# Weight halves side by side and packed operand rows at fixed distances, in a hybrid decoder trunk on one Trainium2 core

## The chip, the cores and the metric

The kernel runs on one core of one Trainium2 chip. The metric is device time in microseconds (us), the median over executions. A core has TensorE (matmuls; PE in the profile, with PEld for its weight loads), VectorE (DVE), ScalarE (ACT), GpSimd (POOL) and SyncE (SP, which here issues the weight DMAs). TensorE reads both operands of a matmul from SBUF, a memory of 128 partitions, and accumulates in PSUM. An address below is a byte address inside one partition; it is the same in all 128.

## The reference

One decoder layer over 16 learned meta tokens and 256 tokens of width 2,048, in float32. A mixer runs two branches side by side on the normalised input, and a squared-ReLU MLP follows.

```python
def hybrid_mixer(xn, w_in, b_forget, w_alpha2, b_alpha, gla_norm_g, w_o_fox, w_o_gla, w_out):
    proj = xn @ w_in
    ...
    o_fox = forgetting_attention(fq, fk, fv, ff, b_forget)
    g_log = jax.nn.log_sigmoid((ga @ w_alpha2 + b_alpha).astype(jnp.float32)) / GLA_TAU
    o_gla = gated_linear_attention(gq, gk, gv, g_log)
    o_gla = (head_rmsnorm(o_gla, gla_norm_g) * jax.nn.silu(gr.astype(jnp.float32))).astype(xn.dtype)
    y = jax.nn.sigmoid(gate_fox) * (o_fox @ w_o_fox) + jax.nn.sigmoid(gate_gla) * (o_gla @ w_o_gla)
    return y @ w_out

def squared_relu_mlp(xn, w1, w2):
    return jnp.square(jax.nn.relu(xn @ w1)) @ w2

def reference(x, ...):
    h = jnp.concatenate([meta, x], axis=1)
    for l in range(DEPTH):          # DEPTH = 1
        h = h + hybrid_mixer(rmsnorm(h, norm_mix_g[l]), ...)
        h = h + squared_relu_mlp(rmsnorm(h, norm_mlp_g[l]), w_ff1[l], w_ff2[l])
    return rmsnorm(h, final_norm_g)[:, N_META:]
```

All large products are [256 or 272 tokens, 2,048] by a weight matrix; w_ff1 and w_ff2 are 2,048 x 8,192 and 8,192 x 2,048.

## The kernel before

Activations lie transposed: features on the partitions, in KT = 16 row tiles of 128, tokens along the free dimension. Weights come as chunks of [2,048 x 128], each 16 blocks of [128 x 128], one block per row tile k; the function `stream` lists the chunks in the order in which they are used.

Precision. Each float32 number is split into an upper part (rounded to the type fp32r) and a lower part (the rest). A product is upper weights by upper and lower activations, plus lower weights by upper activations. In `gemm2` with `mac2` (lines 135 to 146) that is, for each k, one matmul of 512 columns (line 136: upper block by the row's 256 upper and 256 lower columns) and one of 256 columns (line 137: lower block by the 256 upper columns). The text calls these two a pair. A chunk is 16 pairs into one PSUM bank. `gemm_all` (lines 148 to 157) does the same for all 272 tokens in three matmuls of 272 columns. Every matmul loads its own block of weights, while the one before it runs.

Weights. `weight_half` (line 108) takes half a chunk, eight blocks: a DMA into a tile `raw` (line 118, SyncE's queue), a cast to the upper tile on ScalarE (line 120) and a subtraction to the lower tile on VectorE (line 121). Tiles `raw`, `whi` and `wlo` have five buffers each, so these run ahead of TensorE. In `whi` and in `wlo` the eight blocks lie one behind the other, 512 bytes apart. `first_weights` (line 274) does it for the first seven chunks, in eight stages of two row tiles each, and the two tiles `small` (line 357) hold 40 narrow columns in blocks that POOL fills with zeros first (lines 361 and 362). For the last four chunks the upper part goes to a tile of its own, `whi_last` (line 839).

Operands. `operand` (line 221) lays 16 rows into one tile; row k is a place `at` and a step `gap` from its upper to its lower half, both in elements of four bytes:

```python
    S1, S2 = 8728, 8628
    AT_OG = [(540 * k, 264) for k in range(KT)]
    AT_Y = [(544 * k + 16, 256 + 2 * (k // 2)) for k in range(KT)]
    AT_X2 = [(524 * k, 256) for k in range(KT)]
    AT_A = [(544 * k, 256 + 4 * (k // 2)) for k in range(KT)]
```

Four operands go this way: og (the GLA branch's output, for w_o_gla), y (the gated sum, for w_out), x2 (the MLP's normalised input, for w_ff1) and a (the squared ReLU, for w_ff2, made anew for each of the four groups g of 2,048 hidden features). y and a share the tile s1 with x, the mixer's input, whose rows are 272 + 272 elements; og and x2 share s2. The attention branch's output `of` has eight rows of 512 elements and is not among the four.

Order of the work: GLA heads and then attention heads with their projections (x), eight rounds of four gate chunks (x), one chunk for two column tiles of w_o_fox (of) and two chunks of w_o_gla (og), 16 chunks of w_out (y), and four times 16 chunks of w_ff1 (x2) and 16 of w_ff2 (a). TensorE's order is written out by the program; small matmuls of the branches are put between chunks by `later`.

Of the kernel before, what the change touches and what calls it, by code (L numbers as in the profile page):

```python
# [7 lines left out]
F32 = mybir.dt.float32  # L8
F32R = mybir.dt.float32r
# [7 lines left out]
P = 128  # L17
D = 2048
KT = D // P
NM = 16  # L20
NT = 256
# [44 lines left out]
def trunk(ctx: ExitStack, tc: tile.TileContext, hT, w_small, w_all, consts, w_alpha2, out):  # L66
    nc = tc.nc
    serial = [0]

    def nm(s):  # L70
        serial[0] += 1
        return f"{s}_{serial[0]}"

    const = ctx.enter_context(tc.tile_pool(name="const", bufs=1))
    keep = ctx.enter_context(tc.tile_pool(name="keep", bufs=1))
    wp = ctx.enter_context(tc.tile_pool(name="wp", bufs=5))
# [28 lines left out]
    chunk = [0]  # L105
    HK = KT // 2

    def weight_half(c, i, hi=None):

        raw = wp.tile([P, HK * P], F32, tag="raw", name=nm("raw"), bufs=RAW)  # L110
        if hi is None:
            hi = wp.tile([P, HK, P], F32R, tag="whi", name=nm("whi"))
        lo = wp.tile([P, HK, P], F32R, tag="wlo", name=nm("wlo"))

        def step(k0, n):
            k = slice(k0, k0 + n)
            cols = slice(k0 * P, (k0 + n) * P)
            nc.sync.dma_start(raw[:, cols], w_all[c][:, i * HK * P + cols.start : i * HK * P + cols.stop])
            r = raw.rearrange("p (k m) -> p k m", m=P)[:, k, :]
            nc.scalar.copy(hi[:, k, :], r)  # L120
            nc.vector.tensor_tensor(lo[:, k, :], r, hi[:, k, :].bitcast(F32), op=ALU.subtract)  # L121

        return hi, lo, step

    def next_weights(keep_hi=None):
        c = chunk[0]
        chunk[0] += 1
        parts = []
        for i in range(2):
            hi, lo, step = weight_half(c, i, None if keep_hi is None else keep_hi[:, HK * i : HK * (i + 1), :])  # L130
            step(0, HK)
            parts.append((hi, lo))
        return lambda k: (parts[k // HK][0][:, k % HK, :], parts[k // HK][1][:, k % HK, :])
# [5 lines left out]
    def gemm2(w, x, k0=0, nk=KT):  # L139

        ps = bank(pg, "ps")
        for k in range(nk):
            hi, lo = w(k0 + k)
            mac2(ps, hi, lo, x[k], k == 0, k == nk - 1)
        issued()
        return ps
# [12 lines left out]
    def total(ps, t=None):  # L159

        b = tmp.tile([P, NT], F32, tag="evb", name=nm("evb"))
        nc.scalar.copy(b, ps[:, NT:512])
        if t is None:
            t = tmp.tile([P, NT], F32, tag="evt", name=nm("evt"), bufs=4)
        nc.vector.tensor_tensor(t, ps[:, 0:NT], b, op=ALU.add)  # L165
        return t
# [54 lines left out]
    def operand(pool, name, size, places, tag):  # L221


        t = pool.tile([P, size], F32R, tag=tag, name=nm(name))
        rows = []
        for at, gap in places:
            both = t[:, at : at + 2 * gap].rearrange("p (o t) -> p o t", t=gap) if at + 2 * gap <= size else None
            rows.append(both[:, :, 0:NT])
        return rows

    S1, S2 = 8728, 8628
    AT_OG = [(540 * k, 264) for k in range(KT)]
    AT_Y = [(544 * k + 16, 256 + 2 * (k // 2)) for k in range(KT)]
    AT_X2 = [(524 * k, 256) for k in range(KT)]
    AT_A = [(544 * k, 256 + 4 * (k // 2)) for k in range(KT)]


    h = keep.tile([P, KT, NA + 3], F32, name="h")
# [23 lines left out]
    def gain(i, k):  # L262
        return h[:, k, NA + i : NA + i + 1]
# [9 lines left out]

    def first_weights(c0, n, k0):
        raw = wp.tile([P, HK * P], F32, tag="raw", name=nm("raw"), bufs=RAW)
        hi = wp.tile([P, HK, P], F32R, tag="whi", name=nm("whi"))
        lo = wp.tile([P, HK, P], F32R, tag="wlo", name=nm("wlo"))
        r, hi, lo = (t[:, 0 : 2 * n * P].rearrange("p (c k m) -> p c k m", k=2, m=P)
                     for t in (raw, hi.rearrange("p k m -> p (k m)"), lo.rearrange("p k m -> p (k m)")))

        def load(k, nk):
            nc.sync.dma_start(r[:, :, k : k + nk, :],
                              w_all[c0 : c0 + n, :, (k0 + k) * P : (k0 + k + nk) * P].rearrange("c p (k m) -> p c k m", m=P))

        def cut(k, nk):
            ks = slice(k, k + nk)
            nc.scalar.copy(hi[:, :, ks, :], r[:, :, ks, :])
            nc.vector.tensor_tensor(lo[:, :, ks, :], r[:, :, ks, :], hi[:, :, ks, :].bitcast(F32), op=ALU.subtract)

        return hi, lo, load, cut  # L290
# [12 lines left out]
    def load_stage(s):  # L303
        stages[s] = [first_weights(c0, n, 2 * s) for c0, n in ((0, 4), (4, 3))]
        for k in range(2) if s == 0 else (0,):
            for hi, lo, load, cut in stages[s]:
                load(k, 1 if s == 0 else 2)
# [12 lines left out]
    for s in range(KT // 2):  # L320
# [3 lines left out]
        for kk in range(2):  # L324
            k = 2 * s + kk
# [30 lines left out]

    small = []
    for i in range(2):
        hi = wp.tile([P, HK, P], F32R, tag="whi", name=nm("whi"))
        lo = wp.tile([P, HK, P], F32R, tag="wlo", name=nm("wlo"))  # L360
        nc.gpsimd.memset(hi.bitcast(F32), 0.0)
        nc.gpsimd.memset(lo.bitcast(F32), 0.0)
        ws = wsm[:, HK * i : HK * (i + 1), :]
        nc.scalar.copy(hi[:, :, 0:40], ws)
        nc.vector.tensor_tensor(lo[:, :, 0:40], ws, hi[:, :, 0:40].bitcast(F32), op=ALU.subtract)
        small.append((hi, lo))
# [62 lines left out]
    def og_tile():  # L429
        if not og_box:  # L430
            og_box.append(operand(keep, "og", S2, AT_OG, "s2"))
        return og_box[0]
# [307 lines left out]
    for j0 in range(0, KT, 2):  # L740
        gates = ahead if j0 == 0 else [gate() for _ in range(4)]
        w = next_weights()
        for j in range(2):
            t = total(gemm2(w, oft, k0=8 * j, nk=8))
            nc.vector.tensor_tensor(gates[2 * j], gates[2 * j], t, op=ALU.mult)
        for j in range(2):
            t = total(gemm2(next_weights(), og))
            nc.vector.tensor_tensor(t, gates[2 * j + 1], t, op=ALU.mult)
            nc.vector.tensor_tensor(yf[:, j0 + j, :], gates[2 * j], t, op=ALU.add)
    y = operand(keep, "y", S1, AT_Y, "s1")  # L750
    for j in range(KT):
# [5 lines left out]
    ht = h[:, :, NM:NA]  # L757
    x2 = operand(keep, "x2", S2, AT_X2, "s2")

    def square_sum(j, acc):  # L760
        if j == 0:
            nc.scalar.activation(acc, ht[:, j, :], AF.Square)
        else:
            sq = gat.tile([P, NT], F32, tag="hsq", name=nm("hsq"))
            nc.scalar.activation(sq, ht[:, j, :], AF.Square)  # L765
            nc.gpsimd.tensor_tensor(acc, acc, sq, op=ALU.add)  # L766

    def add_residual(j, ps):
        b = tmp.tile([P, NT], F32, tag="evb", name=nm("evb"))
        nc.scalar.copy(b, ps[:, NT:512])  # L770
        nc.vector.tensor_tensor(ht[:, j, :], ps[:, 0:NT], ht[:, j, :], op=ALU.add)
        nc.vector.tensor_tensor(ht[:, j, :], ht[:, j, :], b, op=ALU.add)
# [37 lines left out]
    def relu2(a, f, ps):  # L810
        t = total(ps)
        nc.vector.scalar_tensor_tensor(t, t, 0.0, r2b, op0=ALU.max, op1=ALU.mult)
        s = gat.tile([P, NT], F32, tag="asq", name=nm("asq"))
        nc.vector.tensor_tensor(s, t, t, op=ALU.mult)
        split_to(a[f][:, 0, :], a[f][:, 1, :], s)

    acc = gat.tile([P, NT], F32, tag="acc", name="acc3", bufs=1)
    for g in range(NG):
        a = operand(keep, "a", S1, AT_A, "s1")
        held = []  # L820
        for f in range(KT):
            ps = gemm2(next_weights(), x2)
            if g == 0 and f == 0:
                held.append(ps)
                continue
            if g == 0 and f == 1:
                relu2(a, 0, held.pop())
            relu2(a, f, ps)
        last = g == NG - 1
        for j in range(KT - NL if last else KT):  # L830
            add_residual(j, gemm2(next_weights(), a))
            if last:
                square_sum(j, acc)
                nc.scalar.activation(ht[:, j, :], ht[:, j, :], AF.Identity, scale=gain(2, j))
                if j == 0:
                    tc.keep_in_program_order(nc.scalar.preload_act_table_set("sqrt_and_others"))


    whi = keep.tile([P, NL, KT, P], F32R, tag="s2", name="whi_last")
# [45 lines left out]
    v, p, none = nc.vector, nc.gpsimd, lambda: None  # L885
# [72 lines left out]
```

## Time and profile before

| | |
|---|---|
| median of 3 runs | 1,637.53 us (1,634.11 to 1,637.98) |
| span of the profiled execution, first to last instruction | 1,632.3 us |
| TensorE busy | 1,614.8 us, 99% |
| VectorE, ScalarE, GpSimd busy | 63%, 48%, 6% |
| read from HBM | 289 MB, 178 GB/s over the span |
| pairs of lines 136 and 137 | 3,552 |

The profile gives no time of the profiled execution besides its span; what lies around the span is in the runs' times. A matmul's own duration runs to its modelled end and overlaps the next one, so a rate is read from start to start. In names the buffer numbers are left out: "x" stands for x and for x2, "whi" for all upper weight tiles. Views used: the page (shares, chain, groups), groups kept apart by shape, windows (busy time and number of instructions in a stretch), the timeline, and the waits of an engine.

### The profile page before, as it was taken

How to read it: one execution, taken by the hardware profiler on the slowest of the kernel's cores; microseconds unless marked ns; L12 is line 12 of the kernel's file. 1: busy time of each engine (PE TensorE's matmuls, PEld its weight loads, DVE VectorE, ACT ScalarE, POOL GpSimd, SP SyncE). 2: the span in 40 equal slices, each digit the busy share in tenths (PEclk: the TensorE clock that was granted, in tenths of full speed). 3: DMA queues.
4: the chain of work that ended last, by engine and by line, in shares of the span. 5: the costliest groups of instructions: out<-in, count | busy, mean ns of one | idle time of the engine just before them, and what ended most of it. 6: DMA issues, size and time to landing. Idle time of an engine off the chain costs nothing.

```text
span 1632.3 us, 25617 instructions
## 1 busy us (share of the span) xinstructions
PE 1614.8 (99%) x9996; PEld 1448.8 (89%) x9996; DVE 1033.6 (63%) x1591; ACT 788.5 (48%) x1217; POOL 93.4 (6%) x146
## 2 busy tenths in 40 slices
PE   9999999999999999999999999999999999999997
PEld 7999999999998888888888888888888888888886
DVE  6767657476655555555677766566655776567655
ACT  6555444454445444444555444444444444444563
POOL 1000000010000000000011000000000000000022
PEclk9999999999999999999999999999999999999998
DMA  9444455455455565655555555655566656565662
GB/s 290 143 151 157 159 167 163 160 189 160 157 161 169 187 190 187 188 188 189 188 187 189 185 186 188 188 188 188 181 196 186 191 184 191 187 190 185 188 196 66
DMA packets 90266, 292.97 MB, mean 179 GB/s; under 512 B 9096, under 2 KB 21648, under 8 KB 89888
## 3 DMA queue, kind: packets, MB, share of 16 engines
q1 hardware_dynamic: 87552, 288.88, 55.8%
q8 instruction: 78, 1.28, 0.3%
q10 hardware_dynamic: 2416, 1.33, 0.3%
q0 software_dynamic: 176, 1.12, 0.2%
q14 instruction: 44, 0.36, 0.1%
HBM read 289.19 MB, written 2.11 MB: 178 GB/s over the span
## 4 chain that ended last, share of the span: by engine, by line
PE 97%; DVE 1%; DMA 1%; ACT 0%; issue 0%; SPq 0%; DVEq 0%; ACTq 0%
PE ps L136 50%; PE ps L137 26%; PE psa L155 5%; PE psa L154 5%; PE psa L153 5%; PE ps L854 1%; PE ps L339 1%; DMA h<-hT_dram 1%; PE pa L501 1%; PE ps L845 0%; PE ps L346 0%; PE po L565 0%; DMA raw<-w_all_dram 0%; PE pz L399 0%; PE po L566 0%; PE pq L663 0%
## 5 line engine op out<-in xcount | busy, mean ns | idle before, releaser
L121 DVE TENSOR_TENSOR wlo<-raw,whi 128x1024 fp32r<-128x1024 f32 x522 | 639.9, 1226 | 502.9 <-ACT whi L120 501.3
L120 ACT CAST whi<-raw 128x1024 fp32r<-128x1024 f32 x522 | 547.6, 1049 | 750.9 <-PE ps L136 507.0
L136 PE MATMUL ps<-x,whi 128*128 128x512 f32 x1952 | 688.2, 396 | 0.0
L137 PE MATMUL ps<-x,wlo 128*128 128x256 f32 x1952 | 549.5, 282 | 0.0
L136 PEld LDWEIGHTS ps<-x,whi 128*128 128x128 f32 x1952 | 367.0, 188 | 84.1
L137 PEld LDWEIGHTS ps<-x,wlo 128*128 128x128 f32 x1952 | 368.8, 189 | 0.0
L136 PE MATMUL ps<-a,whi 128*128 128x512 f32 x960 | 336.3, 395 | 0.0
L137 PE MATMUL ps<-a,wlo 128*128 128x256 f32 x960 | 268.5, 280 | 0.0
L136 PEld LDWEIGHTS ps<-a,whi 128*128 128x128 f32 x960 | 180.0, 188 | 42.2
L153 PE MATMUL psa<-x,whi 128*128 128x272 f32 x640 | 187.1, 292 | 2.1 <-DVE ri L196 2.1
L154 PE MATMUL psa<-x,wlo 128*128 128x272 f32 x640 | 184.9, 289 | 0.0
L155 PE MATMUL psa<-x,whi 128*128 128x272 f32 x640 | 184.8, 289 | 0.0
L137 PEld LDWEIGHTS ps<-a,wlo 128*128 128x128 f32 x960 | 181.2, 189 | 0.4
L153 PEld LDWEIGHTS psa<-x,whi 128*128 128x128 f32 x640 | 120.4, 188 | 2.8 <-issue 2.1
L154 PEld LDWEIGHTS psa<-x,wlo 128*128 128x128 f32 x640 | 120.5, 188 | 0.2
L155 PEld LDWEIGHTS psa<-x,whi 128*128 128x128 f32 x640 | 120.6, 188 | 0.1
L136 PE MATMUL ps<-og,whi 128*128 128x512 f32 x256 | 90.3, 395 | 0.0
L136 PE MATMUL ps<-y,whi 128*128 128x512 f32 x256 | 89.8, 395 | 0.0
L766 POOL TENSOR_TENSOR acc<-acc,hsq 128x256 f32<-128x256 f32 x26 | 29.5, 1134 | 775.6 <-ACT hsq L765 775.6
L137 PE MATMUL ps<-og,wlo 128*128 128x256 f32 x256 | 71.8, 281 | 0.0
L137 PE MATMUL ps<-y,wlo 128*128 128x256 f32 x256 | 71.7, 281 | 0.0
L165 DVE TENSOR_TENSOR evt<-ps,evb 128x256 f32<-128x256 f32 x158 | 66.1, 418 | 0.0
(262 smaller groups left out, 1387.0 us busy)
## 6 DMA issues: line engine op xcount, KB each, us to landing
raw<-w_all_dram SPq DMA_DIRECT2D x537, 512.0 KB, 4.3
raw<-w_all_dram SPq DMA_DIRECT2D x7, 384.0 KB, 6.3
h<-hT_dram SPq DMA_DIRECT2D x1, 1100.0 KB, 10.0
negc<-fdram POOLq DMA_DIRECT2D x1, 1088.0 KB, 6.0
out_dram<-h SPq DMA_DIRECT2D x3, 256.0 KB, 2.6
out_dram<-h ACTq DMA_DIRECT2D x3, 256.0 KB, 3.1
h<-hT_dram SPq DMA_DIRECT2D x1, 550.0 KB, 7.3
raw<-w_all_dram SPq DMA_DIRECT2D x2, 256.0 KB, 4.4
```

The costliest lines, as they stand in the source:

```text
L120: nc.scalar.copy(hi[:, k, :], r)
L121: nc.vector.tensor_tensor(lo[:, k, :], r, hi[:, k, :].bitcast(F32), op=ALU.subtract)
L136: nc.tensor.matmul(ps, hi, x, start=first, stop=False)
L137: nc.tensor.matmul(ps[:, 0:NT], lo, x[:, 0, :], start=False, stop=last)
L153: nc.tensor.matmul(ps[:, 0:n], hi, x[:, k, 0, :], start=(k == 0), stop=False)
L154: nc.tensor.matmul(ps[:, 0:n], lo, x[:, k, 0, :], start=False, stop=False)
L155: nc.tensor.matmul(ps[:, 0:n], hi, x[:, k, 1, :], start=False, stop=(k == KT - 1))
L165: nc.vector.tensor_tensor(t, ps[:, 0:NT], b, op=ALU.add)
L339: nc.tensor.matmul(ps, hi, x[:, k, :, NM:NA], start=st, stop=False)
L501: nc.tensor.matmul(dst, k[:, a, :], q[:, a, :], start=(a == 0), stop=(a == 1))
L766: nc.gpsimd.tensor_tensor(acc, acc, sq, op=ALU.add)
L854: nc.tensor.matmul(ps[:, NT:], w(k)[0], a[k][:, :, tok], start=(k == 0), stop=(k == KT - 1))
```

## The change

The upper and lower block of a row tile now lie side by side in one tile of [8 blocks, 2 parts, 128], so that blocks of one part are 1,024 bytes apart and the lower block lies 512 bytes behind its upper one. The five buffers of `whi` and five of `wlo` become five of the joint tile. The rows of og, y, x2 and a become packed: 256 upper and 256 lower elements without a gap, 2,048 bytes, and row k starts at 512 k elements plus an offset that is the same for four row tiles and grows by 64 elements (256 bytes) from each group of four to the next. The first offset is 8, 48 and 40 elements for og, y and x2, and 16, 40, 12 and 58 for a in its four groups g. Zeroing of a `small` tile becomes one memset over both parts. Nothing else is touched: x and of keep their rows, and `whi_last` its blocks.

```diff
+    def pair():
+        return wp.tile([P, HK, 2, P], F32R, tag="wt", name=nm("wt"))
+
     def weight_half(c, i, hi=None):
 
         raw = wp.tile([P, HK * P], F32, tag="raw", name=nm("raw"), bufs=RAW)
+        both = pair()
+        lo = both[:, :, 1, :]
         if hi is None:
-            hi = wp.tile([P, HK, P], F32R, tag="whi", name=nm("whi"))
-        lo = wp.tile([P, HK, P], F32R, tag="wlo", name=nm("wlo"))
+            hi = both[:, :, 0, :]
...
     S1, S2 = 8728, 8628
-    AT_OG = [(540 * k, 264) for k in range(KT)]
-    AT_Y = [(544 * k + 16, 256 + 2 * (k // 2)) for k in range(KT)]
-    AT_X2 = [(524 * k, 256) for k in range(KT)]
-    AT_A = [(544 * k, 256 + 4 * (k // 2)) for k in range(KT)]
+    def steps(first, *by):
+        return [(first + 512 * k + by[k * len(by) // KT], NT) for k in range(KT)]
+
+    AT_OG = steps(8, 0, 64, 128, 192)
+    AT_Y = steps(48, 0, 64, 128, 192)
+    AT_X2 = steps(40, 0, 64, 128, 192)
+    AT_A = [steps(e, 0, 64, 128, 192) for e in (16, 40, 12, 58)]
...
     def first_weights(c0, n, k0):
         raw = wp.tile([P, HK * P], F32, tag="raw", name=nm("raw"), bufs=RAW)
-        hi = wp.tile([P, HK, P], F32R, tag="whi", name=nm("whi"))
-        lo = wp.tile([P, HK, P], F32R, tag="wlo", name=nm("wlo"))
...
+        both = pair()[:, 0 : 2 * n].rearrange("p (c k) o m -> p c k o m", k=2)
+        hi, lo = both[:, :, :, 0, :], both[:, :, :, 1, :]
...
     for i in range(2):
-        hi = wp.tile([P, HK, P], F32R, tag="whi", name=nm("whi"))
-        lo = wp.tile([P, HK, P], F32R, tag="wlo", name=nm("wlo"))
-        nc.gpsimd.memset(hi.bitcast(F32), 0.0)
-        nc.gpsimd.memset(lo.bitcast(F32), 0.0)
+        both = pair()
+        hi, lo = both[:, :, 0, :], both[:, :, 1, :]
+        nc.gpsimd.memset(both.bitcast(F32), 0.0)
...
     for g in range(NG):
-        a = operand(keep, "a", S1, AT_A, "s1")
+        a = operand(keep, "a", S1, AT_A[g], "s1")
```

More of the change, by code (lines that the diff above doesn't have):

```diff
@@ L275, in first_weights @@
         raw = wp.tile([P, HK * P], F32, tag="raw", name=nm("raw"), bufs=RAW)
-        hi = wp.tile([P, HK, P], F32R, tag="whi", name=nm("whi"))
-        lo = wp.tile([P, HK, P], F32R, tag="wlo", name=nm("wlo"))
-        r, hi, lo = (t[:, 0 : 2 * n * P].rearrange("p (c k m) -> p c k m", k=2, m=P)
-                     for t in (raw, hi.rearrange("p k m -> p (k m)"), lo.rearrange("p k m -> p (k m)")))
+        both = pair()[:, 0 : 2 * n].rearrange("p (c k) o m -> p c k o m", k=2)
+        hi, lo = both[:, :, :, 0, :], both[:, :, :, 1, :]
+        r = raw[:, 0 : 2 * n * P].rearrange("p (c k m) -> p c k m", k=2, m=P)
         def load(k, nk):
```

## The prediction

> **What bounds the kernel now.** I read the page first for shares, then its chain, then the stages one by one in windows, then the timeline inside one stage.
>
> ```profile
> span 1632.3 us, 25617 instructions
> PE 1614.8 (99%) x9996; PEld 1448.8 (89%) x9996; DVE 1033.6 (63%) x1591; ACT 788.5 (48%) x1217; POOL 93.4 (6%) x146
> PEclk9999999999999999999999999999999999999998
> ...
> PE 97%; DVE 1%; DMA 1%; ACT 0%; issue 0%; SPq 0%; DVEq 0%; ACTq 0%
> PE ps L136 50%; PE ps L137 26%; PE psa L155 5%; PE psa L154 5%; PE psa L153 5%; PE ps L854 1%; PE ps L339 1%; DMA h<-hT_dram 1%; PE pa L501 1%; PE ps L845 0%; PE ps L346 0%; PE po L565 0%; DMA raw<-w_all_dram 0%; PE pz L399 0%; PE po L566 0%; PE pq L663 0%
> ```
>
> TensorE is the whole time: 97% of the chain, at the full granted clock, and 76% of it are lines 136 and 137, the pair "upper weights by 512 columns, then lower weights by 256". So the change counts by what it does to one such pair. Their number, from the page's groups and the same groups kept apart by shape:
>
> ```profile
> L136 PE MATMUL ps<-x,whi 128*128 128x512 f32 x1952 | 688.2, 396 | 0.0
> L136 PE MATMUL ps<-a,whi 128*128 128x512 f32 x960 | 336.3, 395 | 0.0
> L136 PE MATMUL ps<-og,whi 128*128 128x512 f32 x256 | 90.3, 395 | 0.0
> L136 PE MATMUL ps<-y,whi 128*128 128x512 f32 x256 | 89.8, 395 | 0.0
> L136 PE MATMUL ps<-of,whi 128*128 128x512 f32 x128 | 44.7, 394 | 0.0
> ```
>
> The row "x" mixes two tiles, since numbers are left out of names: 64 chunks of 16 pairs are x2 (1,024), the other 928 are x. The 395 ns are no price: matmuls overlap, so the price is start to start, which a window over a stage with one operand gives. The last column in brackets counts two matmuls still running at the left edge.
>
> ```profile
> 517.53:523.08 5.55, 5.55 (x34) 1.00 0.60 185
> 523.08:534.32 11.24, 11.24 (x66) 1.00 0.62 190
> 534.32:556.72 22.40, 22.40 (x130) 1.00 0.60 187
> 808.68:898.46 89.78, 89.78 (x514) 1.00 0.59 187
> 1078.92:1168.81 89.89, 89.89 (x515) 1.00 0.59 187
> 1168.81:1258.52 89.71, 89.71 (x514) 1.00 0.60 188
> ```
>
> In order these are 16 pairs on of (5.55 / 16 = 346.9 ns), 32 on og (351.3), 64 on x (350.0), 256 on y (350.7), 256 on x2 (351.1), 256 on a (350.4). Same shapes, same clock, no idle: the spread of 4.4 ns is the operand's place. Inside one x2 stage it is larger:
>
> ```profile
> 1300.87 0.28 PE L137 MATMUL ps<-x,wlo 128*128 128x256 f32 x1
> ...
> 1301.23 0.28 PE L137 MATMUL ps<-x,wlo 128*128 128x256 f32 x1
> ...
> 1301.58 0.28 PE L137 MATMUL ps<-x,wlo 128*128 128x256 f32 x1
> ...
> 1301.92 0.28 PE L137 MATMUL ps<-x,wlo 128*128 128x256 f32 x1
> ```
>
> From lower matmul to lower matmul 0.36, 0.35 and 0.34 us, with rows 2,096 bytes apart and weights 512 apart: each row tile has its own rate. These are the outer ends for a pair.
>
> **The change, part by part.** No matmul, weight load, DMA or elementwise pass is added or taken away. What moves is addresses. Bytes within a partition, from the allocation before: upper weights at 127,936 plus multiples of 4,096, lower weights the same from 148,416, tile s1 at 36,928, s2 at 71,840, of at 178,624. The joint tile needs the same 40,960 bytes; I assume it starts at 127,936. Then every upper block lies at 960 and every lower one at 448, modulo 1,024, and a row tile of a changed operand keeps one distance to its weights while k runs over four. Row minus upper block, modulo 1,024: og 256, 512, 768, 0; y 320, 576, 832, 64; x2 384, 640, 896, 128; a 192, 288, 176 and 360 for the four g, each with its steps of 256. Before, the distance changed at every k.
>
> Packed pairs (1,024 of x2, 960 of a, 256 each of y and og). No row shows these distances, so I bound by stages. Operand of already has packed rows, and while k alternates its distances are 0 and 512, two of og's four: 346.9. If all changed pairs ran so: x2 1,024 x 4.2 ns = 4.3 us, a 960 x 3.5 = 3.4, y 256 x 3.8 = 1.0, og 256 x 4.4 = 1.1, together -9.8 us. If all ran as og does now, 351.3: 0.2 + 0.9 + 0.2 = +1.3 us. The outer ends are 0.34 and 0.36 us for each of 2,496 pairs against a mean of 350.8: -27 and +23 us. I take of's rate for og, whose distances are nearest to it (-1.1), and for the others that of x, the other operand whose fine distance to the weights repeats (rows 2,176 and weights 512 apart: the difference is a multiple of 128): 350.0, so x2 -1.1, a -0.4, y -0.2. Sum -2.8 us.
>
> Pairs on x and of, and the 640 triples of lines 153 to 155: the moving rows stay, the weights' pitch goes from 512 to 1,024 bytes. 928 pairs between 346.9 and 351.3 are -2.9 to +1.2 us; the triples are 15% of the chain, some 242 us, and by the same -0.9% and +0.4% -2.2 to +1.0. Nothing favours a sign; I take 0.
>
> Two strided writes, casts and subtractions into 8 blocks of 512 bytes at a pitch of 1,024:
>
> ```profile
> L364 ACT CAST whi<-room x2: 454/458/463, 40.8 to 45.6; 128x320 fp32r<-128x320 f32 x2
> L365 DVE TENSOR_TENSOR wlo<-room,whi x2: 484/488/493, 41.6 to 46.9; 128x320 fp32r<-128x320 f32 x2
> ...
> L121 DVE TENSOR_TENSOR wlo<-raw,whi 128x1024 fp32r<-128x1024 f32 x522 | 639.9, 1226 | 502.9 <-ACT whi L120 501.3
> L120 ACT CAST whi<-raw 128x1024 fp32r<-128x1024 f32 x522 | 547.6, 1049 | 750.9 <-PE ps L136 507.0
> L170 DVE TENSOR_TENSOR a<-asq,a 128x256 fp32r<-128x256 f32 x64 | 26.7, 419 | 0.0
> L169 ACT CAST a<-asq 128x256 fp32r<-128x256 f32 x64 | 25.5, 399 | 0.2 <-DVE asq L814 0.2
> ```
>
> Between 256 and 1,024 contiguous elements ScalarE takes 0.846 ns and VectorE 1.051 ns an element; 320 would be 453 and 486. Lines 364 and 365 write them as eight pieces of 40 at a pitch and take 458 and 488. Gaps cost nothing. Were it 10%, 0.1 us on each of engines that idle half the time.
>
> One buffer in place of two. ScalarE's cast already waits for TensorE to free a slot (the 507.0 us above). A joint slot is freed by the last lower matmul, one 256-column step later, 0.12 us. Five slots of eight pairs are 5 x 2.8 us; cast and subtraction take 2.3, so the next half is ready some 8 us ahead and I cost it at nothing. With that cover gone it would be 0.12 us on each of 522 halves, 63 us. If the program makes upper matmuls wait for the subtraction into the other half of their tile, the same lead hides it.
>
> The prologue has no such lead:
>
> ```profile
> 39.77 0.95 POOL L361 MEMSET whi<- 128x1024 f32 x1 [35.82 <-PE ps L342]
> 40.66 0.96 POOL L362 MEMSET wlo<- 128x1024 f32 x1
> ...
> PE psa L153 <- DVE ri L196: 2.1, 1, 2.1
> ...
> PE ps L339 <- ACT whi L287: 1.3, 1, 1.3
> ```
>
> One memset of twice the width makes the cast behind it start one memset later, 0.95 us, and with it what VectorE has queued ahead of the root for which line 153 waits. Bounds 0 and two such steps, 1.9 us; I take 0.9, once.
>
> Sum: -2.8 + 0.9 = -1.9 us on the profiled span of 1,632.3. The median of the three runs, 1,637.5, lies 5.2 above that span; I carry this over: **1,635.6 us**.
>
> [...] The stages above, 346.9 to 351.3 ns for the same work, speak for some influence of places, though not for one of distances.
> [...]
>
> **The rivals.** (1) Locked in step, faster: a constant distance lets the two reading streams settle where they seldom meet, as on of. All changed pairs at 346.9: 1,637.5 - 9.8 + 0.9 = 1,628.6 us; with x too 1,625.7. For it: of is the only operand with packed rows and the quickest. Against: x2 has packed rows of 2,048 bytes as well, at a pitch of 2,096, and is slow; half of of's speed may be its place.
> (2) Locked in step, slower: what is constant can be constantly bad. x2 has 41% of the changed pairs and only four distances, which share one remainder of 256 bytes. If they settle at 0.36 us, 1,024 x 8.9 ns = +9.1; with the other operands' -1.7 and the prologue's 0.9 that is 1,645.8 us. It turns the sign beyond noise from 356.7 ns a pair of x2 on. For it: 0.36 us occurs in x2 itself. Against: no stage as a whole is above 351.3.
> (3) Nothing: rates depend on neither distance nor packing, and only the prologue pays: 1,638.4 us. For it: four stages lie within 1 ns; against it: of.
>
> **How the numbers follow.** What a measurement of this kernel can tell from no change is about 0.3%, 4.9 us. My forecast, stages that settle between of and x, has 0.32; rival 1 has 0.33, rival 2 0.20, rival 3 0.15. Forecast and rival 3 are within 0.3%: same 0.47, faster 0.33, slower 0.20. The range takes in rivals 1 and 2 and part of the outer ends beyond them, 1,620 to 1,648; the forecast's own range is 1,631 to 1,641.
>
> **What the profile after would show.** Windows over stages of one operand: og at 347, x2, y and a at 350, x at 350. With a constant distance the four starts of a group should be equally spaced, with steps between groups. Cast and subtraction stay at 1,049 and 1,226 ns; ScalarE still waits for line 137 or 136, and TensorE's waits list nothing of line 120 or 121. The prediction is wrong if x2's stage lies outside 347 to 355 ns, if x moves with its weights' pitch, or if TensorE waits for weights.

## The result, and the profile after

Median 1,631.5 us (1,630.7 to 1,631.9) against 1,636.1 us of the kernel before (1,634.0 to 1,638.0), seven runs each: ratio 0.9972, 95% interval 0.9962 to 0.9983. That is 4.6 us faster, just inside the 0.3% that the prediction called noise; the prediction was 1,635.6, and its range of 1,620 to 1,648 holds the time. The interval lies below 1, so with this many runs the small gain is a gain.

The page of the kernel after: span, busy times and chain.

```profile
span 1629.7 us, 25555 instructions
PE 1612.4 (99%) x9996; PEld 1450.3 (89%) x9996; DVE 1048.0 (64%) x1591; ACT 793.7 (49%) x1217; POOL 91.2 (6%) x144
...
PE 98%; DMA 1%; DVE 0%; ACT 0%; issue 0%; SPq 0%; DVEq 0%; ACTq 0%
PE ps L140 50%; PE ps L141 26%; PE psa L159 5%; PE psa L158 5%; PE psa L157 5%; PE ps L345 1%; PE ps L859 1%; DMA h<-hT_dram 1%; PE pa L506 1%; PE ps L850 0%; PE ps L352 0%; PE po L570 0%; DMA raw<-w_all_dram 0%; PE pz L404 0%; ACT x L332 0%; PE po L571 0%
```

Lines 140 and 141 are the old 136 and 137. The bound is the same; what moved is the rate of each stage. Windows of the kernel after (window, its length, TensorE busy, instructions with two still running at the left edge, clock), in order og, x, y, a in group 0, x2, a in groups 1, 2 and 3:

```profile
521.57:532.65 11.08, 11.08 (x66) 1.00 0.59 195
532.65:555.05 22.40, 22.40 (x130) 1.00 0.57 187
805.94:895.25 89.31, 89.31 (x514) 1.00 0.58 194
985.99:1076.43 90.44, 90.44 (x514) 1.00 0.57 187
1076.44:1166.32 89.88, 89.88 (x514) 1.00 0.57 187
1166.33:1255.08 88.75, 88.75 (x514) 1.00 0.58 191
1344.97:1434.56 89.59, 89.59 (x514) 1.00 0.57 188
1524.43:1592.28 67.85, 67.85 (x386) 1.00 0.58 188
```

Per pair: og 346.7 ns (351.4 before), x 350.0 (the same), y 348.9 (350.7), a 353.3, 346.7, 350.0 and 353.4 (350.5), x2 351.1 (the same). Over all chunks that is -1.2 us on og, -0.5 on y, 0.0 on x2 and +0.2 on a: -1.5 us. (These rates, here and below, are means from start to start over all chunks of an operand; one window of a short stage such as og's can differ from them by 0.4 ns.) The group of three matmuls stays at 125.6 ns each.

The steps of 256 bytes from one group of four row tiles to the next, at which the prediction expected the spacing to change, do nothing here. The timeline of the second a (start, duration) at row tiles 3, 7, 11 and 15, so across three borders of groups:

```profile
1167.38 0.39 PE L140 MATMUL ps<-a,wt 128*128 128x512 f32 x1
...
1168.77 0.39 PE L140 MATMUL ps<-a,wt 128*128 128x512 f32 x1
...
1170.15 0.39 PE L140 MATMUL ps<-a,wt 128*128 128x512 f32 x1
...
1171.54 0.39 PE L140 MATMUL ps<-a,wt 128*128 128x512 f32 x1
```

1.39, 1.38 and 1.39 us for four pairs each. If a distance counts modulo 256 only, seven of the 28 are different ones, one for each place in the change, and in this kernel each of these seven has one rate.

The rest of the gain came before the first projection, which begins at 110.2 us of the span instead of 111.8. TensorE's waits in the first 60 us, kernel before and kernel after:

```profile
PE psa L153 <- DVE ri L196: 2.1, 1, 2.1
PE ps L339 <- ACT whi L287: 1.3, 1, 1.3
...
PE ps L339 <- DVE x L327: 0.7, 1, 0.7
```

```profile
PE ps L345 <- ACT wt L293: 3.0, 1, 3.0
...
PE ps L345 <- DVE x L333: 1.0, 1, 1.0
```

The wait for VectorE ahead of the first triple (the group of three matmuls of lines 153 to 155, now 157 to 159) is gone. Two waits in the first stages grew by 2.0 us in these two profiles; in those of the experiments the two come to 1.7 to 4.3 us together, with either kind of weight tile, so this growth is not put down to the change.

### The profile page after: what moved, and what is told of

Its sections match the earlier page's. It is cut to its first block, busy times and chain, and to the rows that moved or that the text cites. A ratio compares the mean times of both kernels' runs of the same rounds, so it can differ in the third digit from the quotient of the medians.

```text
span 1629.7 us, 25555 instructions
## 1 busy us (share of the span) xinstructions
PE 1612.4 (99%) x9996; PEld 1450.3 (89%) x9996; DVE 1048.0 (64%) x1591; ACT 793.7 (49%) x1217; POOL 91.2 (6%) x144
## 4 chain that ended last, share of the span: by engine, by line
PE 98%; DMA 1%; DVE 0%; ACT 0%; issue 0%; SPq 0%; DVEq 0%; ACTq 0%
PE ps L140 50%; PE ps L141 26%; PE psa L159 5%; PE psa L158 5%; PE psa L157 5%; PE ps L345 1%; PE ps L859 1%; DMA h<-hT_dram 1%; PE pa L506 1%; PE ps L850 0%; PE ps L352 0%; PE po L570 0%; DMA raw<-w_all_dram 0%; PE pz L404 0%; ACT x L332 0%; PE po L571 0%
## 5 line engine op out<-in xcount | busy, mean ns | idle before, releaser
L125 DVE TENSOR_TENSOR wt<-raw,wt 128x1024 fp32r<-128x1024 f32 x522 | 644.7, 1235 | 330.0 <-ACT wt L124 320.0
L124 ACT CAST wt<-raw 128x1024 fp32r<-128x1024 f32 x522 | 548.7, 1052 | 397.3 <-issue 158.6
L140 PE MATMUL ps<-x,wt 128*128 128x512 f32 x1952 | 688.4, 395 | 0.0
L141 PE MATMUL ps<-x,wt 128*128 128x256 f32 x1952 | 551.3, 282 | 0.0
L140 PEld LDWEIGHTS ps<-x,wt 128*128 128x128 f32 x1952 | 366.8, 188 | 83.1
L141 PEld LDWEIGHTS ps<-x,wt 128*128 128x128 f32 x1952 | 367.9, 188 | 0.0
L140 PE MATMUL ps<-a,wt 128*128 128x512 f32 x960 | 336.8, 394 | 0.0
L141 PE MATMUL ps<-a,wt 128*128 128x256 f32 x960 | 270.8, 282 | 0.0
L140 PEld LDWEIGHTS ps<-a,wt 128*128 128x128 f32 x960 | 180.7, 188 | 41.0
L157 PE MATMUL psa<-x,wt 128*128 128x272 f32 x640 | 187.3, 293 | 0.0
L159 PE MATMUL psa<-x,wt 128*128 128x272 f32 x640 | 184.8, 289 | 0.0
L158 PE MATMUL psa<-x,wt 128*128 128x272 f32 x640 | 184.4, 288 | 0.0
L141 PEld LDWEIGHTS ps<-a,wt 128*128 128x128 f32 x960 | 181.5, 189 | 0.0
L157 PEld LDWEIGHTS psa<-x,wt 128*128 128x128 f32 x640 | 120.3, 188 | 0.7
L158 PEld LDWEIGHTS psa<-x,wt 128*128 128x128 f32 x640 | 120.4, 188 | 0.2
L159 PEld LDWEIGHTS psa<-x,wt 128*128 128x128 f32 x640 | 120.4, 188 | 0.1
```

What stands on the lines that cost most here:

```text
L140: nc.tensor.matmul(ps, hi, x, start=first, stop=False)
L141: nc.tensor.matmul(ps[:, 0:NT], lo, x[:, 0, :], start=False, stop=last)
L157: nc.tensor.matmul(ps[:, 0:n], hi, x[:, k, 0, :], start=(k == 0), stop=False)
L158: nc.tensor.matmul(ps[:, 0:n], lo, x[:, k, 0, :], start=False, stop=False)
L159: nc.tensor.matmul(ps[:, 0:n], hi, x[:, k, 1, :], start=False, stop=(k == KT - 1))
```

## The experiments

Theories at the start: P, a row's own place modulo 256 bytes sets its rate; D, its distance from the weights does; J, the joint tile gains through the prologue. Three experiments (weights moved by 64 bytes, more distances, a gap) have one run each, of 1,633.9, 1,630.9 and 1,630.6 us, and are read for their stages alone.

**Rows alone.** Weight tiles of before; `steps`, the four places and `AT_A[g]` of the change.

> The packed rows of og, y, x2 and a alone, with upper and lower weights in tiles of their own as before. Theory P (a row's own place modulo 256 bytes sets the rate of its pairs, the weights' place does not): the stages as in the changed kernel, og 346.7 ns a pair, y 348.9, x2 351.1, a 353.3, 346.7, 350.0 and 353.4, and of and x unchanged at 346.7 and 350.0; these are -1.2, -0.5, 0.0 and +0.2 us, so with the prologue of before (first pair of a projection at 111.8 us) some 1.5 us under the kernel before. Theory D (the distance from weights to rows matters, with the weights' pitch of 1,024 bytes): the stages differ from those of the changed kernel by 2 ns or more, since the distance now changes by 512 bytes from k to k. Theory J (the joint tile made the gain, through the prologue): the total equals the kernel before within 0.1%.

1,636.2 us, ratio 1.0001 (0.9992 to 1.0009). og 346.7, x2 351.1, a 353.3, 346.8, 350.0, 353.4, x and of unchanged: the stages are those of the changed kernel, with y alone at 353.1 instead of 348.9. So the weights' pitch (512 or 1,024) is nothing to the rates of the others. That it is what moved y is not shown: y's distance, 64, has both rates within one run further down. The rows alone bring nothing that the runs show (by the stages -0.4 us). J holds for the total.

**Weights alone.** Joint tiles of the change; places of before.

> The joint weight tiles alone, with the rows of og, y, x2 and a as before. Theory P: every stage as before to 0.2 ns (og 351.4, y 350.7, x2 351.1, a 350.5, x 350.0, of 346.7); what is left is the prologue, 1.6 us less if its change is the joint tile's work, so 1,634.5 where before has 1,636. Theory D: the stages of og, y, x2 and a move by 1 ns or more. If the prologue's 1.6 us are chance from run to run, the total is that of before within 0.1%.

1,632.5 us, ratio 0.9977 (0.9968 to 0.9986). Every stage as before to 0.1 ns. So 3.7 of the 4.6 us are the joint tile, more than the 1.6 us that the two profiles differ by in the prologue; the profiled execution of the kernel before, with its span of 1,632.3 us, is one of its fastest. The wait for VectorE was gone here as well.

**Weights moved by 64 bytes.**

```diff
     chunk = [0]
     HK = KT // 2
+    pad = wp.tile([P, 16], F32, tag="pad", name="pad", bufs=1)
+    nc.gpsimd.memset(pad, 0.0)
```

> The changed kernel with a pad of 64 bytes ahead of the weight pool: raw and weight tiles and all that lies behind them, of too, move up by 64 bytes; og, y, x2, a and x stay. Theory P: og 346.7, y 348.9, x2 351.1, a 353.3, 346.7, 350.0, 353.4 and x 350.0 stay to 0.2 ns, while of, whose rows go from 192 to 0 modulo 256, moves from 346.7 to what y has at 0, 348.9. Theory D: of keeps 346.7, since its distance to the weights is kept, and og, y, x2 and a take the rates of distances 64 bytes lower, og for one that of 192 (353.3).

In this kernel (the shifted kernel below) P falls: operands that had not moved changed. Windows of og, y, and a in group 3 (192 pairs):

```profile
520.06:531.35 11.29, 11.29 (x66) 1.00 0.59 190
...
806.73:897.17 90.44, 90.44 (x514) 1.00 0.59 191
...
1528.35:1594.92 66.57, 66.57 (x386) 1.00 0.59 191
```

og 352.8 instead of 346.7, y 353.3 instead of 348.9, the fourth a 346.8 instead of 353.4. That is D, modulo 256: the fourth a now lies 40 bytes behind an upper block, near the 32 of the quick second a. But D's prediction for of failed: moved together with its weights, it went from 346.7 to 352.3. The trace, read from start to start, shows more: this operand has eight stages in the run, and the first has 347.3 ns a pair, the seven others 353.0, with rows and weights in the same places. x2, now at 64, has 348.9 in groups 1 and 2 and 353.3 in group 3. So at 0 and at 64 there are two rates, and one operand can take either in one run.

**All four operands at the distance of the quick one.**

```diff
-    AT_OG = steps(8, 0, 64, 128, 192)
-    AT_Y = steps(48, 0, 64, 128, 192)
-    AT_X2 = steps(40, 0, 64, 128, 192)
-    AT_A = [steps(e, 0, 64, 128, 192) for e in (16, 40, 12, 58)]
+    AT_OG = steps(16, 0, 64, 128, 192)
+    AT_Y = steps(40, 0, 64, 128, 192)
+    AT_X2 = steps(16, 0, 64, 128, 192)
+    AT_A = [steps(e, 0, 64, 128, 192) for e in (40, 40, 40, 40)]
```

> The changed kernel with all four operands at 224 modulo 256, the place that the second a had (346.7 ns a pair). Theory P: x2, y and all four a at 346.7 too, og as it was: x2 1,024 x 4.4 ns = 4.5 us, a (6.6 + 3.3) x 256 and 6.7 x 192 = 3.8 us, y 0.6 us, together 8.9 us less than the changed kernel: 1,622.6 us against its 1,631.5, 0.9917 of the kernel before. A rival: the second a was quick by the phase in which its stage began and not by its place; then some stages stay at 350 to 353 and the gain is under 5 us.

1,621.9 us, ratio 0.9912 (0.9898 to 0.9926), where 1,622.6 was expected. Windows of x2 and of the last a:

```profile
1073.19:1161.92 88.73, 88.73 (x514) 1.00 0.58 190
...
1516.92:1583.47 66.55, 66.55 (x386) 1.00 0.59 192
```

346.6 to 346.7 ns on y, x2 and a, in every stage, so the rival of the expectation falls for this distance; og has 347.1, since its stages of 32 pairs begin with 345, 349, 353 and 352 ns before they settle. Nothing but six numbers in the places differs from the changed kernel, and it saves 9.6 us; it is called the quick kernel below. (It does not yet tell P from D, as both rows and distances agree.)

**The same with the weights moved by 64 bytes,** by the pad above.

> The kernel with all four operands at the quick distance 32, with the weight pool moved up by 64 bytes by a pad and the operands left where they are: the distance becomes 224, which cost 353.3 in the shifted kernel. Theory D: og, y, x2 and all a go from 346.7 to 353.3, which is 2,496 x 6.6 ns = 16.5 us, and of from 346.7 to 352.3, 0.7 us: 1,639 us against 1,621.9 without the pad. Theory P (the rows' own place): 1,622 us.

1,638.1 us, ratio 1.0013 (1.0004 to 1.0022). The window of x2:

```profile
1078.83:1169.28 90.45, 90.45 (x514) 1.00 0.55 186
```

353.3 ns, and 353.2 to 353.4 on all four operands. 64 bytes ahead of the weights, with every one of the four operands in its place, cost 16.2 us: the rows' own place does not set the rate, and the distance does. (That it is not the weights' own place either, the last experiment shows, in which both move.)

**The queue of the prologue.** Tiles and places of before; only the order on ScalarE and VectorE is changed. `freed` holds, for each bank, the copy on ScalarE and the addition on VectorE that empty it (`total`); what is in the `with` block is issued behind those of the first bank.

```diff
+        freed.append((first, second))
...
-    gla_head(0, sg0, (qd0, first_ps[NF - 1]))
+    with tc.issue_after(freed[0][0].ins), tc.issue_after(freed[0][1].ins):
+        gla_head(0, sg0, (qd0, first_ps[NF - 1]))
```

> The kernel before with one thing changed: on ScalarE and VectorE the casts and subtractions of the next chunks are queued behind the first eviction of the prologue's banks, instead of two casts ahead of it. Tiles and rows as before. Theory Q (the joint tile gained through this queue: a later release put the evictions first): TensorE's wait of 2.3 us ahead of the first triple goes below 0.8, the runs lie within about 1 us of each other instead of 4, and the median is near that of the joint tiles with the rows of before, 1,632.5 us against 1,636.2. Rival: the gain is in the tiles' layout; then the median stays within 1 us of 1,636.2.

1,632.5 us (1,631.7 to 1,633.7), ratio 0.9979 (0.9970 to 0.9988): the joint tile's gain without the joint tile. TensorE's wait is gone from its list; the runs lie within 2.0 us of each other, where about 1 was expected. The timeline (start, duration) of ScalarE and VectorE around the first eviction, `evb` and `evt`, in the kernel before, the kernel after, and (ScalarE alone) this one:

```profile
48.87 2.00 ACT L120 CAST whi<-raw 128x1024 fp32r<-128x1024 f32 x2 [2.83 <-PE ps L339]
50.77 0.64 ACT L162 COPY evb<-ps 128x256 f32<-128x256 f32 x2
...
50.11 1.23 DVE L121 TENSOR_TENSOR wlo<-raw,whi 128x1024 fp32r<-128x1024 f32 x1 [2.77 <-ACT whi L120]
...
51.32 1.22 DVE L121 TENSOR_TENSOR wlo<-raw,whi 128x1024 fp32r<-128x1024 f32 x1
52.45 0.42 DVE L165 TENSOR_TENSOR evt<-ps,evb 128x256 f32<-128x256 f32 x1
```

```profile
41.28 1.81 POOL L367 MEMSET wt<- 128x2048 f32 x1 [37.33 <-PE ps L354]
...
50.38 0.65 ACT L166 COPY evb<-ps 128x256 f32<-128x256 f32 x2 [2.25 <-PE ps L352]
50.91 2.01 ACT L124 CAST wt<-raw 128x1024 fp32r<-128x1024 f32 x2
...
50.78 0.76 DVE L169 TENSOR_TENSOR evt<-ps,evb 128x256 f32<-128x256 f32 x2 [1.91 <-ACT evb L166]
```

```profile
50.93 0.37 ACT L164 COPY evb<-ps 128x256 f32<-128x256 f32 x1 [4.30 <-PE ps L349]
51.20 1.05 ACT L120 CAST whi<-raw 128x1024 fp32r<-128x1024 f32 x1
```

Before, two casts on ScalarE and two subtractions on VectorE, for later chunks, stood ahead of the eviction that frees the bank for the first triple: `evt` ended at 52.87 us and the triple began at 53.02. After, the eviction comes first. A joint slot is freed by the last lower matmul and not by the last upper one: the zeroing of the first `small` tile waits for line 354, a lower one, and begins at 41.28 us, where it began at 39.77 behind an upper one (line 342). That this later release is what put the casts behind the eviction is read from the code and these lines and was not varied by itself; that the order is enough for the gain is what the experiment shows.

Why 3.7 us for a wait of 2.1: TensorE's windows of 50 to 53 and 53 to 60 us, in the kernel before and in the one with the rows alone, which has the same wait:

```profile
50.00:53.00 3.00, 0.94 (x10) 1.00 0.20 63
53.00:60.00 7.00, 6.98 (x55) 1.00 0.43 137
```

```profile
50.00:53.00 3.00, 1.08 (x11) 1.00 0.12 37
53.00:60.00 7.00, 6.83 (x42) 0.76 0.44 138
```

In the second the granted clock is 0.76 over 7 us. The clock record in its trace has half clock from 54.5 to 57.9 us, 3.41 us, which costs 1.7 us: 42 instructions instead of 55. The wait ahead of it was 2.1 us, 2.8 with the six one-column matmuls in front; the kernel before has a wait of the same length, and a clock of 1.00 in both windows. So the wait costs its own length, or 1.7 us or more on top, and which one changes from run to run. The runs' own granted clock bears this out: of 51 runs of the kernel before beside the experiments, the 12 up to 1,634.2 us all have 0.997, and the 28 from 1,635.9 us on have 0.995 or 0.994. The kernels without this wait each lie within about 2 us. They can lose clock too, at another wait: the profile of the kernel after has half clock from 22.1 to 25.6 us, 3.41 us again, from the end of the wait of 3.0 us for its early casts (19.6 to 22.55), and that of the kernel with a gap between the halves, further down, from 898.0 to 901.4 us, behind one of 2.0 us for x2. Where the half clock lay in each slower run of before was not seen.

**More distances.** First offsets 48 for og, 36 for y, 22 for x2, and 38, 44, 52, 4 for a.

> The changed kernel with other first offsets, so that the distance from a row to its upper block, modulo 256, is 160 for og, 16 for y, 56 for x2, and 24, 48, 80, 144 for the four a. Theory D256 (the distance modulo 256 sets the rate; known: 32 and 40 give 346.7 ns a pair, 104, 112, 192 and 224 give 353, 176 gives 350.0, 128 gives 351.1, 0 gives 347 or 352, 64 gives 349 or 353): 24 and 48, the neighbours of the quick ones, at 348 or less; the others between 346 and 354. Theory D128 (the period is 128): 160 must be 346.7 as 32 is, and 48 must be 350.0 as 176 is.

160: 346.8; 16: 346.7; 24: 359.9; 48: 350.0; 80: 353.3; 144: 346.6; 56: 346.7 or 353.3. The windows of the a at 24 and of x2 at 56 in group 1:

```profile
983.72:1075.85 92.13, 92.13 (x514) 1.00 0.55 184
1075.86:1166.30 90.44, 90.44 (x514) 1.00 0.55 186
```

The guess that neighbours of 32 are quick was wrong: 24 is the slowest of all, 13 ns above 16 and 32. x2 at 56 has 353.3 in this stage and in that of group 2, but 346.7 in that of group 3 (88.75 us for 256 pairs), at the same distance in the same run. So the rival that came up with the quick kernel, that the state in which a stage begins counts, is out at 32 and alive at 0, 56 and 64. A period of 128 fits three couples (16 and 144, 32 and 160, 48 and 176 have the same rate); 0 and 128 do not fit it, since 128 gave 351.1 on x2 and, in the shifted kernel, on the first a, and 0 never did. D128 stays open.

**A gap between the halves.** Upper halves at distance 32, lower halves 16 x 1,024 bytes and some more behind.

```diff
...
+        first, far = places
+        both = t[:, first : first + 2 * far].rearrange("p (o t) -> p o t", t=far)
+        rows = [both[:, :, NT * k : NT * (k + 1)] for k in range(KT)]
...
```

> All four operands with their upper halves one behind the other at a pitch of 1,024 bytes, at distance 32 from the upper weights, and their lower halves far behind, so that from upper to lower half it is, modulo 256, 128 bytes for og, 64 for y, 192 for x2, and 32, 96, 160, 224 for the four a (0 in the kernel with the quick distance). If the upper half alone sets the rate, all stay at 346.7 ns a pair. If the lower half's distance counts as well, the 512-column matmul moves and the 256-column one stays at 118; rates between 343 and 357, and a gap below 346.7 would be a version to build on.

Extra gap 64, 96, 160: 346.7; 192: 347.8; 32, 128, 224: 353.1 to 353.3. The lower half's place counts, and none of these is below 346.7. As expected in that case it is the 512-column matmul that moves: from its start to the next one it takes 228.5 ns at 96 and 234.2 at 32, the 256-column one 118.2 and 119.1.

**Apart, in the right order, at distance 32.** The queue of the experiment above and the places of the quick kernel, with weight tiles apart.

> Neither joint tiles nor 28 distances: weight tiles apart as before, the next chunks' casts queued behind the prologue's first eviction, and all four operands in packed rows at distance 32. If the two effects are independent and the joint tile is not needed for either: 1,632.45 us of the kernel with the queue alone, less og 4.7 ns x 256, y 4.1 x 256, x2 4.4 x 1,024 and a 3.8 x 960, together 10.4 us: 1,622.0 us, the same as the joint tiles at that distance (1,621.9). If side by side is what makes a constant distance work, the operands' stages differ from 346.7 ns and the total is 1,625 or more.

1,622.2 us, ratio 0.9922 (0.9908 to 0.9935), the operands at 346.7 to 347.1. Both effects add up and neither needs the halves side by side.

**Distance of x.** The quick kernel, pad of 8 elements, places 8 elements up.

> The kernel at distance 32 (1,621.9 us) with a pad of 32 bytes ahead of the weight pool and the four operands moved up by the same 32 bytes. Their distance stays 32; that of x, whose 928 pairs alternate between 192 and 64, becomes 160 and 32. If only the distance counts, x goes from 350.0 to 346.7 ns as every packed operand did at 160 and at 32: -3.1 us; the four operands stay at 346.7; the triples on x, 125.6 ns a matmul, may move by 1 ns either way, 1.9 us; of, moved together with its weights, by up to +0.7 us as in the kernel shifted by 64: 1,617 to 1,621.5 us. If x's rate is set by its pitch, it stays at 350.0 and the total at 1,622.

1,625.0 us, ratio 0.9938 (0.9926 to 0.9951): a miss. The four operands stayed at 346.7 to 346.9, though rows and weights had both moved by 32, which is D again. But x went to 352.7, not 346.7. For x, whose rows are 2,176 bytes apart and whose distance alternates, the rates of constant distances do not hold.

The version that beats both kernels is the one at distance 32, with joint tiles (1,621.9) or with the order written out (1,622.2).

## Why the prediction was right, point by point

The forecast, within 0.3% and a little faster, came out, but for other reasons than its own sum of -2.8 and +0.9: the runs put the first part at -1.5 and the second, which had the wrong sign, at -3.7. That the two errors partly cancel is luck. None of the prediction's own signs of being wrong appeared: x2 stayed at 351.1, x at 350.0, and TensorE waits for no weights behind the prologue.

- *Packed pairs, -2.8 us.* Measured -1.5. og got of's rate, 346.7, as forecast (-1.1 predicted, -1.2 measured). The reason given, of's distances, is half of it: at distance 0 y ran at 353.3 and of itself mostly at 353.0 in the shifted kernel, so that og took the quicker of two rates is luck. For x2 (-1.1), a (-0.4) and y (-0.2) the step "take x, the other operand whose fine distance repeats" failed: a constant distance does not pull a stage to 350. a's four groups lie at 346.7, 350.0 and twice 353.4, a mean near the old one. That x2 gained nothing and a lost a little comes from which distances modulo 256 were picked.
- *Ends of the bounds.* -9.8 us for all at of's rate was a good end: with all four at the quick distance the pairs gained 10.4 us against the kernel before, at 346.7 to 347.1. The other end, all at 351.3, was too low: whole stages at 353.3 and 359.9 exist. The timeline inside one stage (0.34 to 0.36) had said so.
- *x, of and the triples, 0.* Right: a pitch of 1,024 for 512 changed them by less than 0.1 ns.
- *Strided writes, nothing.* Right: cast 1,052 ns (1,049), subtraction 1,235 (1,226).

```profile
L125 DVE TENSOR_TENSOR wt<-raw,wt 128x1024 fp32r<-128x1024 f32 x522 | 644.7, 1235 | 330.0 <-ACT wt L124 320.0
L124 ACT CAST wt<-raw 128x1024 fp32r<-128x1024 f32 x522 | 548.7, 1052 | 397.3 <-issue 158.6
```

- *Joint slots hidden.* Right in the steady part: TensorE's one listed wait for a weight tile, 3.0 us, ends at 22.6 us of the span.
- *The prologue, +0.9 us, bounds 0 and 1.9.* Wrong in sign and size: -3.7 us in the medians. The step that failed is "makes the cast behind it start one memset later, and with it what VectorE has queued ahead of the root". Later casts did come, but they no longer stood ahead of the eviction, and the wait they caused went away. The prediction had bounded a delay of the casts without asking who stood behind them. It also took the profile's label at its word: line 153 was said to wait for the root on VectorE, but by the code the first triple reads nothing of the root and needs the bank that the eviction beside it frees.
- *5.2 us around the span.* Not a constant: in every run that lists its span the time is about 1.7 above it (the kernel after 1,631.4 beside a span of 1,629.7). The other 3.5 were the spread among the runs of before, whose profiled execution was one of the fastest.
- *Rival 1* (settles on of's rate) holds for og and the second a, *rival 2* (locks on a slow rate) for two of the a; x2 was neither. *Rival 3* (places do nothing) is refuted by the two kernels with the pad. Moving the weights of the quick kernel by 64 bytes changed 2,496 pairs by some 6.6 ns, from 346.7 to 353.3. That reading streams meet or miss each other, as rival 1 has it, no run here shows.

## What to carry to other kernels

When TensorE is busy 99% of the span, ask for the rate per matmul by stage: here operands of one shape differed by up to 13 ns in 347, and six numbers in a layout were worth 9.6 us. Before a layout is trusted, vary one distance at a time and hold it for whole stages, and read each stage by itself: mixed distances hide good and bad ones in one mean, and so do stages that took different rates at one distance. And a buffer that is freed a little later can be a gain (3.7 us here), when what it delays stood in a queue ahead of something urgent.

## What the runs showed of the hardware

At a constant distance the stages of these runs had few rates. All of them by stage, in bytes from the upper block to the row, modulo 256, packed rows, with kernels that show them:

| rate, ns a pair | distances | seen in |
|---|---|---|
| 346.6 to 346.8 | 16, 32, 40, 144, 160 | More distances (16, 144, 160), the quick kernel (32), the shifted kernel (40) |
| 350.0 | 48, 176 | More distances (48), the changed kernel (176) |
| 351.1 | 128 | the changed kernel (x2), the shifted kernel (the first a) |
| 353.3 or 353.4 | 80, 104, 112, 192, 224 | More distances (80), the changed kernel (104, 192), the shifted kernel (112, 224) |
| 359.9 | 24 | More distances |
| two rates | 0 (346.7 or 353.0 to 353.3), 56 (346.7 or 353.3), 64 (348.9 or 353.1 to 353.3) | the changed and the shifted kernel (0, 64), Rows alone (64), More distances (56) |

The short stages of og differ by up to 0.5 with their first pairs: 347.1 at 32 and, in the shifted kernel, 352.8 at 192. 346.7, 353.3 and 359.9 are 6.6 apart, and no stage of these operands lies below 346.6. The rates between are mixtures, read from start to start: the a at 176 alternates between 354 and 346 ns, and x2 at 128 repeats 346, 354 and 353.

At 0, 56 and 64 one operand took both rates in different stages of one run (of, x2 and x2), so the distance does not set the rate alone there; the state in which a stage begins is a candidate that was not varied. What the step of 6.6 ns comes from, and why x had other rates (350.0, and 352.7 in the last experiment), stays open: no run here shows a mechanism.
